# Layer 1 of a hybrid encoder: PSUM evacuation of the S5 states split over two engines, and the scan cut into two halves of the groups

## The chip, the cores and the metric

The kernel runs on one core of one Trainium2 chip. The metric is the device time of one execution in microseconds (us); lower is better. Engines are named as in the profile: PE (matmul), PEld (its weight loads), DVE (vector), ACT (scalar), POOL and SP (here they mostly issue DMAs).

## What is computed

Two encoder layers over 272 tokens (256 and 16 meta tokens) of width 2048. Each has a mixer and a channel mixer (layer 0 a dense SwiGLU, layer 1 a top-2-of-8 mixture of experts). The mixer projects the normed input once, gives one part to latent attention of 8 heads and the other, `u`, to a bidirectional S5, whose core is

```
bu = jnp.einsum('gpc,blgc->blgp', b_bar, u_c)
def combine(left, right):
    a_l, b_l = left
    a_r, b_r = right
    return a_r * a_l, a_r * b_l + b_r
_, h = lax.associative_scan(combine, (a, bu), axis=1, reverse=reverse)
return jnp.real(jnp.einsum('gcp,blgp->blgc', c, h))
```

for 64 groups of 16 channels with 64 complex states, forward and backward. Its output goes through a gelu and a gate (GLU); both halves are normed and multiplied by `w_out`.

## The kernel before

All weights stream through SBUF in 128x1024 blocks (`raw`), which ACT rounds into `wh` and DVE subtracts into `wl`; each product is three matmuls (XH·wh, XL·wh, XH·wl).

The S5 in chunks: tokens come in 68 chunks of 4. `ssm_x` (L1033) makes for each of 32 pairs of groups (one from each half of the 64) the state inputs of all chunks by matmuls into one PSUM bank, and ACT copies them into the tile `X` [128 partitions, 67 chunks, re/im, 64 groups] in two instructions: the forward direction in partitions 0 to 63, the backward one, in reversed order of chunks, in 64 to 127. `ssm_scan` (L1076) then steps over the 66 chunks: four DVE instructions a step, two products with `L8` (the transition, prepared at the end of `prep`, L811) and two adds into `X[:, s]`. `ssm_h` (L1094) copies states out of `X` in 16 pieces H (ACT the forward half, DVE the backward half), `ssm_y` (L1270) multiplies them on PE with the output weights (24 matmuls for each of 8 row tiles T, in the order 0, 4, 1, 5, 2, 6, 3, 7), copies the result `y` out, transposes it on PE, and ACT makes the gelu and its rounded copy for the GLU. Both `ssm_h` and `ssm_y` wait for the flag `("scan", l)`, `ssm_h` also for `("att", l)`, the end of attention. In the trace almost all these tiles are called `fa` (one arena); `L` is `L8`, `ra` the rounded arena.

Order of the work: nothing is reordered on the chip; each engine runs its queue in order. The queues are written by a planner when the kernel is built. A main generator (`mixer`, L1386) writes the big matmuls of a layer: projections of `u` (8 row tiles), of q and kv, the heads, then the first half of `w_out` (`w_out`, L1596, 16 blocks of 24 matmuls, each with two DVE instructions `tmpr` and `h`), then it waits for the flag `("Y", l)`, and only then the GLU. Side generators (attention and the `ssm_` functions) are let in between by a model of the engines' clocks: a scan step is written only when

```
return self.m.t["DVE"] < self.now() + self.lead[w]
```

that is, when DVE's planned time is less than 1200 ns ahead of PE's, and one that waits for data only when the planned time of the data is past. So the more planned DVE work there is, the later the scan's last step stands relative to the main matmuls.

Of the kernel before, what the change touches and what calls it, by code (L numbers as in the profile page):

```python
# [12 lines left out]
AF = mybir.ActivationFunctionType  # L13
OP = mybir.AluOpType
# [50 lines left out]

def rows(t, off, ap):
    return bass.AP(tensor=t.tensor, offset=t.offset + off, ap=ap)


class Arena:  # L70
# [461 lines left out]
class Kern:  # L532
# [278 lines left out]
    def prep(self, l, F):  # L811
# [103 lines left out]
        for b in range(0, len(src), 8):  # L915
            bank = yield from self.grab()
            ps = bank.rearrange("p (s g) -> p s g", g=64)
            part = src[b:b + 8]
            for i, (s, m, r) in enumerate(part):
                nc.tensor.transpose(ps[:, i, :], s, idn)  # L920
            i = 0
            while i < len(part):
                j = i
                while j + 1 < len(part) and part[j + 1][2] == part[i][2] and (part[j + 1][1] < n1) == (part[i][1] < n1):
                    j += 1
                m0, r, n = part[i][1], part[i][2], j - i + 1
                if m0 < n1:
                    nc.vector.tensor_copy(self.Wp[0:64, r, m0:m0 + n], ps[0:64, i:i + n])
                    hi = n1 - m0
                    nc.vector.tensor_copy(self.Wp[64:128, r, hi - n + 1:hi + 1], ps[64:128, i + n - 1:(i - 1 if i else None):-1])  # L930
                elif r == 0:
                    nc.vector.tensor_copy(self.L8[:, 0, 0], ps[:, i])
                    nc.vector.tensor_copy(self.L8[:, 0, 1], ps[:, i])
                else:
                    nc.vector.tensor_copy(self.L8[:, 1, 1], ps[:, i])
                    nc.vector.tensor_scalar(self.L8[:, 1, 0], ps[:, i], -1.0, None, op0=OP.mult)
                i = j + 1
            self.drop(bank)
            yield f"prep{l}"
# [93 lines left out]
    def ssm_x(self, l, F):  # L1033

        nc, st = self.nc, self.st
        X = st["X"]
        st["xu"] = {}

        def inputs():
            for qb in range(4):  # L1040
                yield lambda: qb - st["xb"] < 2
                yield self.has("u", l, qb)
                yield self.has("u", l, qb + 4)
                yield max(self.rdy(self.uscr[l][qb]), self.rdy(self.uscr[l][qb + 4]))
                u = self.load_u(l, qb)
                st["xu"][qb] = u, self.rdy(u)

        st["xb"] = 0
        self.s.add(inputs())
        for qb in range(4):  # L1050
            yield lambda: qb in st["xu"]
            u, t = st["xu"][qb]
            yield t
            for q in range(0, 8, VG):
                yield lambda: len(st["vq"]) > 0
                v, t = st["vq"].pop(0)
                yield t
                for i in range(VG):
                    g = qb * 8 + q + i
                    bank = yield from self.grab()  # L1060
                    ps = bank[:, :4 * NC].rearrange("p (r h s) -> p r h s", r=2, h=2)
                    for r in range(2):
                        nc.tensor.matmul(ps[:, r].rearrange("p h s -> p (h s)"), v[:, i, r],
                                         u[:, q + i].rearrange("p h s -> p (h s)"), start=True, stop=True)
                    if i == VG - 1:
                        st["vn"] += 1
                    yield None
                    nc.scalar.activation(X[0:64, :, :, g::NQ].rearrange("p s r h -> p r h s"),
                                         ps[0:64, :, :, 0:NC - 1], AF.Copy)
                    nc.scalar.activation(X[64:128, ::-1, :, g::NQ].rearrange("p s r h -> p r h s"),  # L1070
                                         ps[64:128, :, :, 1:NC], AF.Copy)
                    self.drop(bank)
            st["xb"] = qb + 1
        self.flags.add(("X", l))

    def ssm_scan(self, l, F):  # L1076
        nc, st = self.nc, self.st
        TT = nc.vector.tensor_tensor
        yield self.has("X", l)
        X = st["X"]  # L1080
        yield self.rdy(X.ap)
        t1, t2 = F.get([2, NG], top=True), F.get([2, NG], top=True)
        for s in range(1, NC - 1):
            TT(t1.ap, self.L8[:, 0], X[:, s - 1], op=OP.mult)
            TT(t2.ap, self.L8[:, 1], X[:, s - 1, ::-1], op=OP.mult)
            TT(X[:, s], X[:, s], t1.ap, op=OP.add)
            TT(X[:, s], X[:, s], t2.ap, op=OP.add)
            yield f"scan{l}"
        t1.free()
        t2.free()  # L1090
        st["tX"] = self.rdy(X.ap)
        self.flags.add(("scan", l))

    def ssm_h(self, l, F):  # L1094
# [10 lines left out]
        for T in TORD:  # L1105
            for a in (0, 4):
                yield lambda: n - st["hn"] < 2
                t = rh.next()
                yield self.s.m.clear(t)
                g = 8 * T + a  # L1110
                nc.scalar.activation(t[0:64, :, :, 1:NC],
                                     X[0:64, :, :, g:g + 4].rearrange("p s r g -> p g r s"), AF.Copy)
                nc.vector.tensor_copy(t[64:128, :, :, 0:NC - 1],
# [1264 lines left out]
```

## Time and profile before

| | us |
|---|---|
| median of 3 runs (2504.59 to 2511.16) | 2509.04 |
| the profiled execution | 2510.87 |
| its span, first to last instruction | 2509.1 |
| PE busy in the span | 2426.2 |
| DVE busy | 1903.8 |
| ACT busy | 1397.2 |

The profiled execution's time is 1.8 us above its span and 1.8 us above the median. Busy PE is matmuls with modelled ends. In layer 1's mixer the state inputs are made until 1383 us of the span, the scan runs from 1383 to 1519.5, the softmax of attention from 1450, first half of `w_out` from 1514 with the S5 output inside it, GLU from 1591.

### The profile page before, as it was taken

The page shows a single profiled execution, that of the slowest core. Times are in us where ns is not written, and L with a number is a line of the kernel's source. Part 1 is how long each engine was busy: PE and PEld are TensorE (multiplying, and loading weights), DVE is VectorE, ACT ScalarE, POOL GpSimd, SP SyncE. Part 2 cuts the span into 40 slices and gives each one's busy share as a digit, 9 for nine tenths or more (in the row PEclk, how much of TensorE's full clock was granted, in tenths as well). Part 3 has the DMA queues.
Part 4 walks back from the last instruction along what each step waited for, and adds up shares of the span by engine and source line. Part 5 has one row for each costly group of instructions (what it writes and reads, how often), then busy time and mean ns, then how long its engine had stood idle before and what let it go on. Part 6 is the DMA issues. An engine that isn't in the chain of part 4 may idle for free. (4 is left out here: it accounts for less than half of the span.)

```text
span 2509.1 us, 42278 instructions
## 1 busy us (share of the span) xinstructions
PE 2426.2 (97%) x15930; PEld 2185.7 (87%) x15930; DVE 1903.8 (76%) x3250; ACT 1397.2 (56%) x1908; POOL 152.1 (6%) x263
## 2 busy tenths in 40 slices
PE   8889999999999999999999799999999999999997
PEld 6676699999999999999998768997888888888886
DVE  7788667787766666555663987758999999999997
ACT  4324656443333333333448457547777777877775
POOL 4400100011100000000011002000000000000000
PEclk9999999999999999999999999999999999999998
DMA  7842454568855655555565325667999999999995
GB/s 246 240 134 92 138 161 152 168 211 269 260 187 192 193 193 187 171 174 176 173 197 190 101 68 161 224 228 266 389 347 355 384 339 376 362 330 372 362 336 198
DMA packets 192807, 583.47 MB, mean 233 GB/s; under 512 B 36097, under 2 KB 48769, under 8 KB 191441
## 3 DMA queue, kind: packets, MB, share of 16 engines
q1 hardware_dynamic: 174802, 520.42, 59.5%
q0 software_dynamic: 17072, 58.03, 7.6%
q8 instruction: 127, 2.08, 0.3%
q10 hardware_dynamic: 720, 2.23, 0.2%
q14 instruction: 86, 0.70, 0.1%
HBM read 560.14 MB, written 22.54 MB: 232 GB/s over the span
## 5 line engine op out<-in xcount | busy, mean ns | idle before, releaser
L408 DVE TENSOR_TENSOR wl<-raw,wh 128x1024 fp32r<-128x1024 f32 (+1 forms) x559 | 667.6, 1203 | 223.3 <-ACT wh L408 199.3
L408 ACT ACTIVATE wh<-raw 128x1024 fp32r<-128x1024 f32 (+1 forms) x559 | 579.3, 1040 | 315.0 <-PE bank L408 221.4
L408 PE MATMUL bank<-XH,wh 128*128 128x272 f32 (+1 forms) x2160 | 637.8, 295 | 0.8 <-ACT tmpr L408 0.5
L408 PE MATMUL bank<-XH,wl 128*128 128x272 f32 (+1 forms) x2160 | 623.7, 289 | 5.2 <-DVE wl L408 5.2
L408 PE MATMUL bank<-XL,wh 128*128 128x272 f32 (+1 forms) x2160 | 622.1, 288 | 1.6 <-DVE XL L408 1.3
L408 PEld LDWEIGHTS bank<-XH,wl 128*128 128x128 f32 x2160 | 408.0, 189 | 6.5 <-DVE wl L408 6.5
L408 PEld LDWEIGHTS bank<-XH,wh 128*128 128x128 f32 x2160 | 408.6, 189 | 5.2 <-ACT tmpr L408 0.7
L408 PEld LDWEIGHTS bank<-XL,wh 128*128 128x128 f32 x2160 | 408.7, 189 | 2.7 <-DVE XL L408 2.2
L408 PE MATMUL bank<-ra,wh 128*128 128x272 f32 (+1 forms) x1792 | 342.6, 291 | 2.3 <-ACT wh L408 2.3
L408 PEld LDWEIGHTS bank<-ra,wh 128*128 128x128 f32 x1792 | 281.9, 189 | 7.7 <-issue 3.1
L408 PE MATMUL bank<-fa 128*68 128x64 f32 (+12 forms) x1892 | 254.9, 273 | 26.2 <-ACT fa L408 7.9
L408 DVE TENSOR_TENSOR fa<-fa 128x128 f32<-128x128 f32 (+9 forms) x687 | 236.2, 353 | 40.3 <-ACT fa L408 15.8
L408 PEld LDWEIGHTS bank<-fa 128*68 128x68 f32 (+6 forms) x1892 | 190.9, 157 | 84.8 <-issue 43.8
L408 PE MATMUL bank<-ra,wl 128*128 128x272 f32 (+1 forms) x896 | 257.3, 287 | 0.8 <-DVE wl L408 0.8
L408 ACT ACTIVATE fa<-bank 64x268 f32<-64x268 f32 (+9 forms) x313 | 159.4, 515 | 154.6 <-PE bank L408 128.0
L408 PE MATMUL bank<-wh,XH 128*128 128x512 f32 (+1 forms) x584 | 222.4, 381 | 0.7 <-ACT fa L408 0.4
L408 PE MATMUL bank<-wh,XL 128*128 128x512 f32 (+1 forms) x584 | 220.5, 378 | 0.0
L408 PE MATMUL bank<-wl,XH 128*128 128x512 f32 (+1 forms) x584 | 219.1, 375 | 0.0
L408 PE MATMUL bank<-wh,ra 128*128 128x512 f32 x552 | 185.2, 392 | 0.0
L408 PE MATMUL bank<-fa,raw 128*128 128x272 f32 x608 | 164.5, 408 | 8.9 <-ACT fa L408 8.9
L408 PEld LDWEIGHTS bank<-ra,wl 128*128 128x128 f32 x896 | 169.3, 189 | 1.0 <-DVE wl L408 1.0
L408 DVE TENSOR_TENSOR wl<-h,wh 128x1024 fp32r<-128x1024 f32 (+1 forms) x137 | 157.0, 1156 | 10.0 <-ACT wh L408 7.5
(128 smaller groups left out, 3213.1 us busy)
## 6 DMA issues: line engine op xcount, KB each, us to landing
raw<-w_dense SPq DMA_DIRECT2D x264, 512.0 KB, 3.5
raw<-w_mix SPq DMA_DIRECT2D x150, 512.0 KB, 3.4
raw<-w_moe_g SPq DMA_DIRECT2D x106, 512.0 KB, 5.4
h<-w_moe_g SPq DMA_DIRECT2D x80, 512.0 KB, 5.6
raw<-w_moe_d SPq DMA_DIRECT2D x73, 512.0 KB, 6.6
h<-w_moe_d SPq DMA_DIRECT2D x59, 512.0 KB, 6.3
raw<-w_moe_t SPq DMA_DIRECT2D x51, 384.0 KB, 4.2
h<-w_moe_t SPq DMA_DIRECT2D x44, 384.0 KB, 3.9
```

The costliest lines, as they stand in the source:

```text
L408: return f(*a, **k)
```

## The change

The 64 columns of `X` and `L8` get another order: 16 columns belong to one of the four quarters of the groups' pairs, so the first two quarters fill columns 0 to 31. `L8` is written in that order (layer 0 too), and `ssm_h` reads by it. In layer 1 DVE, instead of ACT, copies the backward half out of PSUM, and the scan is two passes over 32 columns each; the first may start when two quarters of `X` are there. Layer 0 keeps one pass and ACT alone.

```diff
@@ prep @@
-                    nc.vector.tensor_copy(self.L8[:, 0, 0], ps[:, i])
-                    nc.vector.tensor_copy(self.L8[:, 0, 1], ps[:, i])
+                    nc.vector.tensor_copy(by_use(self.L8[:, 0, 0]), by_half(ps[:, i]))
+                    nc.vector.tensor_copy(by_use(self.L8[:, 0, 1]), by_half(ps[:, i]))
...
@@ ssm_x @@
-                    nc.scalar.activation(X[0:64, :, :, g::NQ].rearrange("p s r h -> p r h s"),
+                    c = slice(qb * 16 + q + i, qb * 16 + 16, 8)
+                    nc.scalar.activation(X[0:64, :, :, c].rearrange("p s r h -> p r h s"),
                                          ps[0:64, :, :, 0:NC - 1], AF.Copy)
-                    nc.scalar.activation(X[64:128, ::-1, :, g::NQ].rearrange("p s r h -> p r h s"),
-                                         ps[64:128, :, :, 1:NC], AF.Copy)
+                    back = X[64:128, ::-1, :, c].rearrange("p s r h -> p r h s")
+                    if l:
+                        nc.vector.tensor_copy(back, ps[64:128, :, :, 1:NC])
+                    else:
+                        nc.scalar.activation(back, ps[64:128, :, :, 1:NC], AF.Copy)
                     self.drop(bank)
             st["xb"] = qb + 1
+            self.flags.add(("X", l, qb))
@@ ssm_scan @@
-        t1, t2 = F.get([2, NG], top=True), F.get([2, NG], top=True)
-        for s in range(1, NC - 1):
-            TT(t1.ap, self.L8[:, 0], X[:, s - 1], op=OP.mult)
-            TT(t2.ap, self.L8[:, 1], X[:, s - 1, ::-1], op=OP.mult)
-            TT(X[:, s], X[:, s], t1.ap, op=OP.add)
-            TT(X[:, s], X[:, s], t2.ap, op=OP.add)
-            yield f"scan{l}"
+        n = NG // 2 if l else NG
+        for a in range(0, NG, n):
+            yield self.has("X", l, (a + n) // 16 - 1)
+            X, L8 = st["X"][:, :, :, a:a + n], self.L8[:, :, :, a:a + n]
+            yield self.rdy(X)
+            t = [F.get([2, n], top=True) for _ in range(2)]
+            for s in range(1, NC - 1):
+                for i, x in enumerate((X[:, s - 1], X[:, s - 1, ::-1])):
+                    nc.vector.tensor_tensor(t[i].ap, L8[:, i], x, op=OP.mult)
+                for x in t:
+                    nc.vector.tensor_tensor(X[:, s], X[:, s], x.ap, op=OP.add)
+                yield f"scan{l}"
...
@@ ssm_h @@
-                g = 8 * T + a
+                g = T % 4 * 16 + T // 4 * 8 + a
```

The queues of SP and POOL are the same before and after. DVE has 296 instructions more (32 copies, 264 of the scan), ACT 32 fewer, PE as many as before; PE's queue differs only in layer 1's mixer. The lines move by 9 (L408 is now L417). Two places:

**PE, first half of layer 1's `w_out`** (`XH,wh`, `XL,wh`, `XH,wl` are its matmuls, 128x256; `fa 68x64` those of `ssm_y`, `cst,fa 128x68` its transposes, `ra,wh` the GLU). Before:

```order
L408 MATMUL bank_66<-XH,wh_101 128x256
L408 MATMUL bank_66<-XL,wh_101 128x256
L408 MATMUL bank_66<-XH,wl_104 128x256
L408 MATMUL bank_69<-fa 68x64 x6
L408 MATMUL bank_70<-cst,fa 128x68 x4
L408 MATMUL bank_66<-XH,wh_101 128x256
```

After, the end of `w_out`'s last block and the beginning of what follows it:

```order
L417 MATMUL bank_66<-XH,wh_101 128x256
L417 MATMUL bank_66<-XL,wh_101 128x256
L417 MATMUL bank_66<-XH,wl_104 128x256
L417 MATMUL bank_71<-fa 68x64 x24
L417 MATMUL bank_69<-fa 68x64 x12
L417 MATMUL bank_70<-cst,fa 128x68 x4
L417 MATMUL bank_69<-fa 68x64 x12
L417 MATMUL bank_68<-fa 68x64 x12
```

and the end of that stretch:

```order
L417 MATMUL bank_68<-fa 68x64 x12
L417 MATMUL bank_70<-fa 68x64 x12
L417 MATMUL bank_69<-cst,fa 128x68 x4
L417 MATMUL bank_70<-fa 68x64 x12
L417 MATMUL bank_71<-cst,fa 128x68 x4
L417 MATMUL bank_67<-ra,wh_102 128x256 x2
L417 MATMUL bank_67<-ra,wl_105 128x256
```

Before, `ssm_y`'s 192 matmuls stand in sixes between threes of `w_out`, from its fourth block on, and 210 matmuls of `w_out` follow them. Now all 384 matmuls of `w_out` come first, then all of `ssm_y` with nothing between, then the GLU.

**DVE at the end of the scan** (`fa<-L_93,fa` are a step's two products, `fa<-fa` its two adds; `tmpr` and `h` belong to a block of `w_out`; `MEMSET fa` and `COPY fa<-fa` are the beginning of `ssm_h`). Before, the last step and what follows:

```order
L408 TENSOR_TENSOR wl_106<-raw_97,wh_103 128x1024
L408 TENSOR_TENSOR fa<-L_93,fa 128x128 x2
L408 TENSOR_TENSOR fa<-fa 128x128 x2
L408 MEMSET fa 128x544 x2
L408 RECIPROCAL fa<-fa 128x256
L408 TENSOR_TENSOR tmpr<-bank_66,fa 128x256
L408 TENSOR_TENSOR h<-h,tmpr 128x256
```

After, the last two blocks of `w_out` with the steps between:

```order
L417 TENSOR_TENSOR tmpr<-bank_65,fa 128x256
L417 TENSOR_TENSOR h<-h,tmpr 128x256
L417 TENSOR_TENSOR wl_106<-raw_97,wh_103 128x1024
L417 TENSOR_TENSOR fa<-L_93,fa 128x64 x2
L417 TENSOR_TENSOR fa<-fa 128x2x32 x2
L417 TENSOR_TENSOR tmpr<-bank_66,fa 128x256
L417 TENSOR_TENSOR h<-h,tmpr 128x256
L417 TENSOR_TENSOR fa<-L_93,fa 128x64 x2
```

The last step stood ahead of the RECIPROCAL that opens `w_out`'s DVE work. Now 105 of the 132 half-width steps stand ahead of that RECIPROCAL, 12 stand one by one behind blocks 4 to 15 of `w_out`, and 15 in a row behind the last one, ahead of the MEMSET. Of the 105, 22 stand ahead of DVE's work on the second block of the q projection (the row that ran at 1379.58 us, behind which the scan used to begin), with 29 of the 32 PSUM copies; 83 steps and 3 copies stand from there to the RECIPROCAL, where all 66 full-width steps stood.

## Rows read from the trace of the kernel before

**Rows 1.** The page, part 1: busy us (share of the span) xinstructions, by engine.

```profile
PE 2426.2 (97%) x15930; PEld 2185.7 (87%) x15930; DVE 1903.8 (76%) x3250; ACT 1397.2 (56%) x1908; POOL 152.1 (6%) x263
```

**Rows 2.** Busy time of each engine by stretch of layer 1's mixer: stretch, its length, busy us (and instructions) of PE, PEld, DVE, ACT, POOL, granted TensorE clock as a share of 2.4 GHz, DMA share, GB/s.

```profile
1330.00:1383.00 53.00, 49.65 (x400) 48.44 (x399) 18.09 (x20) 44.52 (x64) 7.63 (x13) 1.00 0.56 182
1383.00:1450.00 67.00, 52.52 (x339) 47.78 (x339) 61.88 (x169) 28.10 (x47) 0.00 (x0) 0.95 0.33 108
1450.00:1500.00 50.00, 46.42 (x242) 31.81 (x242) 41.71 (x158) 30.36 (x82) 0.00 (x0) 1.00 0.21 68
1500.00:1516.00 16.00, 15.62 (x49) 9.12 (x49) 14.38 (x60) 6.94 (x18) 1.77 (x3) 0.58 0.02 5
...
1523.00:1568.50 45.50, 43.25 (x543) 42.04 (x542) 28.93 (x44) 34.13 (x45) 7.36 (x11) 1.00 0.55 171
```

**Rows 3.** What PE waited for from 1383 to 1520 us: waiting engine and tile, releaser, us in total, times, longest; the rows released by DVE.

```profile
PE bank L408 <- DVE wl L408: 6.7, 5, 2.2
PE bank L408 <- DVE fa L408: 5.5, 3, 2.4
PE bank L408 <- DVE XL L408: 4.0, 4, 1.9
```

**Rows 4.** The same from 1300 to 1383 us, the first row.

```profile
PE bank L408 <- ACT fa L408: 3.8, 5, 1.0
```

**Rows 5.** DVE in order of time near the scan's beginning: start, us, instruction, count (instructions in a row are merged): one step of 128 elements and the next one's products.

```profile
1384.06 0.49 DVE L408 TENSOR_TENSOR fa<-L,fa 128x128 f32<-128x128 f32 x2
1384.47 0.61 DVE L408 TENSOR_TENSOR fa<-fa 128x128 f32<-128x128 f32 x2
1385.12 0.49 DVE L408 TENSOR_TENSOR fa<-L,fa 128x128 f32<-128x128 f32 x2
```

**Rows 6.** DVE's instructions of the whole span by form: shapes, count, then busy us and mean ns of one, then idle time before them. The first is a scan step's add, the third a plain copy out of PSUM, the fourth the copies of `ssm_h`, which read `X` in steps of one chunk.

```profile
L408 DVE TENSOR_TENSOR fa<-fa 128x128 f32<-128x128 f32 x264 | 76.0, 288 | 4.6
...
L408 DVE TENSOR_TENSOR fa<-fa 128x16 f32<-128x16 f32 x6 | 1.0, 172 | 0.1
...
L408 DVE COPY fa<-bank 128x256 f32<-128x256 f32 x8 | 3.3, 413 | 0.0
...
L408 DVE COPY fa<-fa 64x536 f32<-64x536 f32 x32 | 24.3, 780 | 1.1 <-PE bank L408 0.4
```

**Rows 7.** ACT by form from 1320 to 1383 us, the copies of the states out of PSUM (all 64 of layer 1).

```profile
L408 ACT ACTIVATE fa<-bank 64x268 f32<-64x268 f32 x64 | 41.1, 642 | 8.0 <-PE bank L408 7.0
```

**Rows 8.** PE in order of time: the first matmul of `w_out`'s first half, a sum of squares among them, and the first matmul of the GLU.

```profile
1514.23 0.38 PE L408 MATMUL bank<-XH,wh 128*128 128x256 f32 x1
...
1517.46 0.70 PE L408 MATMUL bank<-fa,ones 128*128 128x256 f32 x2
...
1591.37 0.40 PE L408 MATMUL bank<-ra,wh 128*128 128x256 f32 x2
```

**Rows 9.** DVE in order of time behind `ssm_y`, while PE does `w_out` alone: one block's `tmpr` and `h`, and the next block's `tmpr`.

```profile
1571.69 0.43 DVE L408 TENSOR_TENSOR tmpr<-bank,fa 128x256 f32<-128x256 f32 x1 [0.64 <-PE bank L408]
1572.15 0.42 DVE L408 TENSOR_TENSOR h<-h,tmpr 128x256 f32<-128x256 f32 x1
...
1574.53 0.42 DVE L408 TENSOR_TENSOR tmpr<-bank,fa 128x256 f32<-128x256 f32 x1 [0.64 <-PE bank L408]
```

**Rows 10.** DVE at the scan's end: the last step's adds and the memsets of `ssm_h`.

```profile
1518.86 0.61 DVE L408 TENSOR_TENSOR fa<-fa 128x128 f32<-128x128 f32 x2
1519.54 1.08 DVE L408 MEMSET fa<- 128x544 f32 x2
```

**Rows 11.** ACT, the first H copy.

```profile
1520.08 1.18 ACT L408 ACTIVATE fa<-fa 64x536 f32<-64x536 f32 x1 [0.46 <-DVE fa L408]
```

**Rows 12.** PE inside `ssm_y`: a run of its matmuls (24 records are the 12 matmuls of one H, two records each) and the transposes of one T.

```profile
1533.31 1.64 PE L408 MATMUL bank<-fa 128*68 128x64 f32 x24
...
1537.45 0.42 PE L408 MATMUL bank<-cst,fa 68*128 68x68 f32 x4
```

**Rows 13.** ACT through one T of `ssm_y`: y copy, H copy, gelu, rounded copy, then (left out, 1.14 us) another H copy, next y copy.

```profile
1540.59 0.59 ACT L408 ACTIVATE fa<-bank 68x512 f32<-68x512 f32 x1 [0.54 <-PE bank L408]
1541.08 1.15 ACT L408 ACTIVATE fa<-fa 64x536 f32<-64x536 f32 x1
1543.13 0.63 ACT L408 ACTIVATE fa<-bank 128x256 f32<-128x256 f32 x1 [0.90 <-PE bank L408]
1543.79 0.42 ACT L408 ACTIVATE ra<-fa 128x256 fp32r<-128x256 f32 x1
...
1545.40 0.59 ACT L408 ACTIVATE fa<-bank 68x512 f32<-68x512 f32 x1 [0.15 <-PE bank L408]
```

**Rows 14.** Busy time by stretch, columns as in rows 2: two pieces of attention.

```profile
1460.00:1470.00 10.00, 9.16 (x49) 6.11 (x47) 8.71 (x31) 6.35 (x18) 0.00 (x0) 1.00 0.24 73
1500.00:1510.00 10.00, 10.00 (x23) 5.11 (x23) 8.62 (x37) 3.97 (x12) 0.00 (x0) 0.50 0.00 0
```

**Rows 15.** PE behind a wait of 2.34 us that ended at 1397.32: two matmuls of one form.

```profile
1398.97 0.43 PE L408 MATMUL bank<-XH,wh 128*128 128x272 f32 x1
...
1401.06 0.29 PE L408 MATMUL bank<-XL,wh 128*128 128x272 f32 x1
```

**Rows 16.** Sum over 1600 to 1750 us, the stretch from the GLU to the first experts, columns as in rows 2.

```profile
sum 150.00, PE 141.71 PEld 129.49 DVE 104.02 ACT 83.58 POOL 4.78; mean PE 47.24 PEld 43.16 DVE 34.67 ACT 27.86 POOL 1.59
```

More of the change, by code (lines that the diff above doesn't have):

```diff
@@ L67, in rows, with by_half, by_use @@
     return bass.AP(tensor=t.tensor, offset=t.offset + off, ap=ap)
+def by_half(t):
+    return t.rearrange("p (h q i) -> p h q i", h=2, q=4)
+def by_use(t):
+    return t.rearrange("p (q h i) -> p h q i", h=2, q=4)
 class Arena:
@@ L931, in prep @@
                 elif r == 0:
-                    nc.vector.tensor_copy(self.L8[:, 0, 0], ps[:, i])
-                    nc.vector.tensor_copy(self.L8[:, 0, 1], ps[:, i])
-                else:
-                    nc.vector.tensor_copy(self.L8[:, 1, 1], ps[:, i])
-                    nc.vector.tensor_scalar(self.L8[:, 1, 0], ps[:, i], -1.0, None, op0=OP.mult)
+                    nc.vector.tensor_copy(by_use(self.L8[:, 0, 0]), by_half(ps[:, i]))
+                    nc.vector.tensor_copy(by_use(self.L8[:, 0, 1]), by_half(ps[:, i]))
+                else:
+                    nc.vector.tensor_copy(by_use(self.L8[:, 1, 1]), by_half(ps[:, i]))
+                    nc.vector.tensor_scalar(by_use(self.L8[:, 1, 0]), by_half(ps[:, i]), -1.0, None, op0=OP.mult)
                 i = j + 1
@@ L1058, in ssm_x @@
                 for i in range(VG):
-                    g = qb * 8 + q + i
                     bank = yield from self.grab()
@@ L1077, in ssm_scan @@
         nc, st = self.nc, self.st
[L1078 to L1081, printed above, removed]
-        t1, t2 = F.get([2, NG], top=True), F.get([2, NG], top=True)
-        for s in range(1, NC - 1):
-            TT(t1.ap, self.L8[:, 0], X[:, s - 1], op=OP.mult)
-            TT(t2.ap, self.L8[:, 1], X[:, s - 1, ::-1], op=OP.mult)
-            TT(X[:, s], X[:, s], t1.ap, op=OP.add)
-            TT(X[:, s], X[:, s], t2.ap, op=OP.add)
-            yield f"scan{l}"
-        t1.free()
-        t2.free()
-        st["tX"] = self.rdy(X.ap)
+        n = NG // 2 if l else NG
[10 more added lines that the diff above has]
+                yield f"scan{l}"
+            for x in t:
+                x.free()
+        st["tX"] = self.rdy(st["X"].ap)
         self.flags.add(("scan", l))
```

## The prediction, made before the changed kernel ran

> **What bounds the kernel now.** I read the page's first part first: PE is busy for 97% of the span [rows 1], so a change can win only where PE idles, and it loses whatever idle time it adds to PE. The next view is the table by stretch [rows 2]; the reader is to see where layer 1's mixer leaves PE idle: 3.35 us while the states are made (1330 to 1383), then 14.48, 3.58 and 0.38 us up to 1516, and 2.25 us in the stretch of `ssm_y` (1523 to 1568.5). The waits name the releasers: from 1383 to 1520 DVE ended 6.7 + 5.5 + 4.0 = 16.2 us of PE's waits [rows 3], and before that ACT, which copies the states out, ended 3.8 [rows 4]. From 1383 to 1516 DVE is busy 118 of 133 us, with the scan in it. So the change attacks two real waits. What it does to the order behind them weighs more: `ssm_y` ran inside `w_out`, and PE was busy 43.25 of those 45.5 us [rows 2].
>
> **The prices.** A full-width step starts 1.06 us after the one before (1384.06 to 1385.12 [rows 5]), with four instructions. One of 128 elements takes 288 ns, one of 16 takes 172 [rows 6]: 1.036 ns an element over a fixed 155 ns, so one of 64 takes 222. Four times 66 ns less makes a half-width step 0.79 us. It can't cost more than the full one, 1.06, nor less than half, 0.53. A pass over all groups is 66 x 1.06 = 70 us before, 132 x 0.79 = 104 us after: DVE gets 34 us more. The row nearest in kind to DVE's copy out of PSUM is 413 ns for 256 elements [rows 6]; ACT's takes 642 for 268 [rows 7], as ACT pays for the stepped side; DVE's copies of `ssm_h`, stepped too, take 780 for 536, close to the plain rate. I take 0.45 us, between 0.41 and 0.64: 32 x 0.45 = 14 us more on DVE, 32 x 0.64 = 20.5 us less on ACT. The different column order of `L8` and of the copies keeps their counts and sizes; I cost it at nothing.
>
> **Term 1, the states.** ACT's share per bank falls from two copies to one, so the 3.8 us [rows 4] can go. On DVE, 29 copies (13 us) and 22 steps (17 us) now stand before the point of 1379.58; some eight of the copies fall before 1330, so the stretch holds 18 + 27 = 45 of 53 us of DVE work. That fits, though a copy can stand behind a step or a `wl` and hold a bank. I take -2, with ends -3.8 (all of the wait) and +6 (a bank held 0.8 us by a step for eight groups).
>
> **Term 2, projections and attention.** Where 66 steps (70.0 us) stood, 83 half-width ones stand (65.6 us), with 3 copies more (1.4) and without the memsets (1.1): DVE has 4 us less of 118. Of the 16.2 us that PE waits for DVE I let 2 go: -2. Ends: -4, all of it passed on, and 0.
>
> **Term 3, the scan's tail and `ssm_y`.** PE's queue now holds all of `w_out`'s first half, then all of `ssm_y`, then the GLU. `w_out` begins at 1514.23 [rows 8]; a block takes 2.84 us (1571.69 to 1574.53 [rows 9]); 16 blocks are 45.4, with 0.7 for the sum among them [rows 8], so PE is through at 1560.3. The steps behind blocks 4 to 15 fit: 0.42 + 0.42 + 1.22 + 0.79 with the `wl` is 2.85 of 2.84. After the last `tmpr` and `h` (1.0 with the hand-over) DVE has 15 steps left: 15 x 0.79 = 11.9, to 1573.2, while PE stands, since nothing else is in its queue. The last add to ACT's first H copy was 0.61 (1519.47 to 1520.08) and the copy 1.18 [rows 10, 11]; with a hand-over the first matmul of `ssm_y` is at 1575.2.
>
> From there `ssm_y` runs alone. Per T PE has 2 x 1.64 for the matmuls and 0.42 for the transposes [rows 12], 3.70; ACT has 0.59 + 1.15 + 0.63 + 0.42 + 1.14 = 3.93 [rows 13]; DVE, two copies of 0.78 and one 0.42, has slack. They wait for each other: the transposes wait for the y copy and stand behind the next H's matmuls, and ACT's gelu waits for them. I walk that ring: two sets of matmuls, the transposes, one y copy and a hand-over of 0.1 make 4.4 us, between 3.70 (PE alone) and 4.81 (1540.59 to 1545.40 with `w_out` in between [rows 13]). First T: two sets, y copy and hand-overs, 4.2 us, and 1.7 more because PE comes out of a long wait: behind 2.34 us of waiting a matmul took 0.43, 2 us later 0.29 [rows 15], starts 0.23 and 0.12 apart. Then 7 x 4.4 = 30.8, and the last T's transposes, gelu, rounded copy and subtraction, 0.42 + 0.63 + 0.42 + 0.42 with 0.5 of hand-overs, 2.4. The GLU starts at 1575.2 + 5.9 + 30.8 + 2.4 = 1614.3, not at 1591.37 [rows 8]: **+22.9 us**. Ends: cycles at 3.70 and 4.81, -4.9 and +2.9.
>
> What stands behind the GLU is unchanged and PE-bound, so the delay stays. Sum: -2 - 2 + 22.9 = +18.9 on the profiled 2510.87; against the median, 1.8 us lower, 2509.0 + 18.9 = **2528 us**.
>
> **A rule against the change.** In the trace two independent products take 0.49 us together where one alone takes 0.285, so the second starts before the first has ended [rows 5]. The Trainium skill, "VectorE: DVE Perf Modes", section "The DRAIN you can't avoid", says the next operation does not start until the pipeline is empty, and its rules for authors say to keep the number of operations low. By that rule the doubled count of scan instructions would cost more than I take; the trace bears the overlap out instead, for these products at least.
>
> **Rivals.**
> - *Steps dearer*: the four instructions don't overlap at half width and take 4 x 0.222 = 0.89 us, and PSUM copies take ACT's 0.64. Term 2 gets 83 x 0.10 = 8 us and term 3 15 x 0.10 = 1.5, term 1 turns to +6 because the copies hold banks: 2528 + 18 = 2546. Against it the overlap in rows 5, for it the short adds that depend on each other (0.61 for two). 0.13.
> - *`ssm_y` at the half clock*: PE at 1.2 GHz doubles its share of the ring, 4 x 1.64 + 0.84 + 0.69 = 8.1, so 7 x 3.7 = 26 us more: 2554. For it: the tail of attention, where PE stands between short bursts, ran at 0.50 [rows 14]. Against it: at 1460 to 1470 PE, with its weight loads busy 6.1 of 10 us, had 1.00, and alone in `ssm_y` it would have 3.7 of 4.4. The Trainium skill, "TensorE: Matmul & The Clock Gate", "Part 1: The HAM clock gate", says that the low level is the default and sustained work releases it; the rows fit that. 0.10.
> - *The delay is taken back later*: from 1600 to 1750 PE idles 150 - 141.7 = 8.3 us [rows 16]; if all of it were late data that now has time to come, the time is 2520. Nothing shows that these waits are for data. 0.08.
> - *Not slower*: a half-width step costs half, 0.53 us. Then term 2 frees 70 - 44 = 26 us of DVE, and all 16.2 us of PE's waits for DVE go (14 more than taken), ACT's wait goes too (2), the tail is 15 x 0.26 = 4 shorter, and the ring runs at PE's 3.70 (5 less): 2528 - 25 = 2503. It decides below about 0.6 us a step. Against it stands the fixed part in rows 6: 172 ns for 16 elements. 0.06.
> - *The change doesn't do what it says*: the first pass does start earlier, the second ends later, so the scan as a whole ends later; that is my forecast.
>
> **Chances.** Forecast 0.63, the rivals 0.13, 0.10, 0.08 and 0.06. Its own range is 2509 + 18.9 - 4.9 - 1.8 - 2 = 2519 to 2528 + 2.9 + 2 + 8 = 2541. To leave out no more than 0.2 I go down to 2516 and up to 2547, which takes in the dearer steps and the delay taken back; the half clock and the other side stay out. A difference of 0.3%, 7.5 us, is about what a measurement of this kernel can tell from none: faster 0.04 (half of the last rival and some luck), same 0.07, slower 0.89.
>
> **What would show it.** Right: scan instructions `fa<-L` 128x64, 0.22 us each; ACT's copies of 64x268 halved; a gap on PE of about 15 us between the last XH matmul of `w_out`'s first half and the first 128x64 one, ended by DVE or ACT `fa`; then some 37 us in which PE is busy well under 90% with no XH matmul; GLU 20 us later. Wrong: a gap under 8 us, `ssm_y` in under 30 us, or a stretch 1383 to 1516 shorter by 10 us.

## The result: slower by 0.86%

| | before | after |
|---|---|---|
| median, us | 2508.87 (6 runs, 2504.59 to 2512.82) | 2530.82 (6 runs, 2528.78 to 2536.22) |
| ratio to before, 95% interval | | 1.0086 [1.0071, 1.0102], that is +18 to +26 us |
| the profiled execution, us | 2510.87 | 2528.78 |
| its span, us | 2509.1 | 2527.0 |

The forecast was 2528, slower. The profiled execution is the shortest of the six, 2 us under their median, so what its trace adds up to (+17.9) stands a little under the difference of the medians (+22).

The page's first part, to be read beside [rows 1]: PE does the same work in a longer span, DVE is busy 46 us more (the forecast had 34 for the scan and 14 for the copies), ACT 23 less.

```profile
PE 2424.0 (96%) x15930; PEld 2187.6 (87%) x15930; DVE 1949.5 (77%) x3546; ACT 1374.6 (54%) x1876; POOL 152.6 (6%) x263
```

The table by stretch of layer 1's mixer, the same columns as [rows 2]. The last two stretches are new: the gap, and `ssm_y` by itself.

```profile
1330.00:1383.00 53.00, 48.64 (x395) 47.66 (x394) 44.94 (x131) 27.02 (x38) 7.40 (x12) 1.00 0.55 172
1383.00:1450.00 67.00, 54.92 (x337) 49.26 (x336) 61.42 (x209) 27.48 (x48) 0.00 (x0) 0.92 0.37 117
1450.00:1500.00 50.00, 47.27 (x247) 32.04 (x245) 41.21 (x191) 31.41 (x88) 0.00 (x0) 1.00 0.17 55
1500.00:1516.00 16.00, 12.94 (x77) 10.99 (x78) 15.23 (x65) 8.10 (x15) 5.54 (x9) 0.89 0.51 153
1555.10:1569.80 14.70, 0.03 (x1) 0.02 (x1) 13.52 (x67) 1.42 (x2) 0.00 (x0) 0.60 0.12 37
1569.80:1607.50 37.70, 31.15 (x415) 30.32 (x416) 13.87 (x22) 27.88 (x38) 7.49 (x11) 0.88 0.34 100
```

DVE's and ACT's work moves as planned (26.9 us more and 17.5 less from 1330 to 1383), but for PE the stretches up to 1500 look as before: where the change was to help, its busy time moves by 1 to 2.4 us up or down. From 1555.1 to 1569.8 PE does nothing while DVE is busy 13.5 of 14.7 us, and in the 37.7 us after that PE is busy 31.2.

PE in order of time (compare [rows 8, 12]): the first matmul of `w_out`, its last one, the first of `ssm_y`, one cycle of it, the last transposes, the first of the GLU.

```profile
1507.47 0.58 PE L417 MATMUL bank<-XH,wh 128*128 128x256 f32 x1
...
1554.85 0.28 PE L417 MATMUL bank<-XH,wl 128*128 128x256 f32 x1
1569.81 7.10 PE L417 MATMUL bank<-fa 128*68 128x64 f32 x72 [14.67 <-ACT fa L417]
...
1600.32 0.42 PE L417 MATMUL bank<-cst,fa 68*128 68x68 f32 x4
1600.57 1.64 PE L417 MATMUL bank<-fa 128*68 128x64 f32 x24
1603.21 1.66 PE L417 MATMUL bank<-fa 128*68 128x64 f32 x24 [1.00 <-ACT fa L417]
1604.71 0.42 PE L417 MATMUL bank<-cst,fa 68*128 68x68 f32 x4
...
1607.29 0.47 PE L417 MATMUL bank<-cst,fa 68*128 68x68 f32 x4 [0.68 <-ACT fa L417]
1607.56 0.48 PE L417 MATMUL bank<-ra,wh 128*128 128x256 f32 x2
```

The wait of 14.67 us is put down to ACT, whose H copy came last. DVE and ACT show who was late: behind the last block's `h` DVE goes through 15 steps in a row (first and last shown), then the memsets, and ACT's H copy had itself waited 15.11 us for DVE.

```profile
1555.63 0.42 DVE L417 TENSOR_TENSOR h<-h,tmpr 128x256 f32<-128x256 f32 x1
1555.97 0.35 DVE L417 TENSOR_TENSOR fa<-L,fa 128x64 f32<-128x64 f32 x2
1556.24 0.48 DVE L417 TENSOR_TENSOR fa<-fa 128x64 f32<-128x64 f32 x2
1556.76 0.36 DVE L417 TENSOR_TENSOR fa<-L,fa 128x64 f32<-128x64 f32 x2
...
1567.29 0.48 DVE L417 TENSOR_TENSOR fa<-fa 128x64 f32<-128x64 f32 x2
1567.83 1.09 DVE L417 MEMSET fa<- 128x544 f32 x2
```

```profile
1568.38 2.10 ACT L417 ACTIVATE fa<-fa 64x536 f32<-64x536 f32 x2 [15.11 <-DVE fa L417]
```

The prices, by form (columns of [rows 6]): the adds and products of a half-width step, and DVE's copies out of PSUM.

```profile
L417 DVE TENSOR_TENSOR fa<-fa 128x64 f32<-128x64 f32 x264 | 58.5, 222 | 4.5
...
L417 DVE TENSOR_TENSOR fa<-L,fa 128x64 f32<-128x64 f32 x264 | 47.1, 220 | 2.3
...
L417 DVE COPY fa<-bank 64x268 f32<-64x268 f32 x32 | 18.3, 638 | 9.1 <-ACT fa L417 8.8
```

### The profile page after: what moved, and what is told of

Its sections match the earlier page's. It is cut to its first block, busy times and chain, and to the rows that moved or that the text cites. A ratio compares the mean times of both kernels' runs of the same rounds, so it can differ in the third digit from the quotient of the medians.

```text
span 2527.0 us, 42564 instructions
## 1 busy us (share of the span) xinstructions
PE 2424.0 (96%) x15930; PEld 2187.6 (87%) x15930; DVE 1949.5 (77%) x3546; ACT 1374.6 (54%) x1876; POOL 152.6 (6%) x263
## 5 line engine op out<-in xcount | busy, mean ns | idle before, releaser
L417 DVE TENSOR_TENSOR wl<-raw,wh 128x1024 fp32r<-128x1024 f32 (+1 forms) x559 | 667.6, 1202 | 191.7 <-ACT wh L417 186.4
L417 ACT ACTIVATE wh<-raw 128x1024 fp32r<-128x1024 f32 (+1 forms) x559 | 579.7, 1040 | 332.5 <-PE bank L417 246.6
L417 PE MATMUL bank<-XH,wh 128*128 128x272 f32 (+1 forms) x2160 | 636.6, 295 | 0.8 <-ACT tmpr L417 0.5
L417 PE MATMUL bank<-XH,wl 128*128 128x272 f32 (+1 forms) x2160 | 625.0, 289 | 5.3 <-DVE wl L417 5.3
L417 PE MATMUL bank<-XL,wh 128*128 128x272 f32 (+1 forms) x2160 | 623.7, 289 | 1.5 <-DVE XL L417 1.3
L417 PEld LDWEIGHTS bank<-XH,wl 128*128 128x128 f32 x2160 | 409.6, 190 | 6.2 <-DVE wl L417 6.2
L417 PEld LDWEIGHTS bank<-XH,wh 128*128 128x128 f32 x2160 | 410.1, 190 | 5.3 <-ACT tmpr L417 0.7
L417 PEld LDWEIGHTS bank<-XL,wh 128*128 128x128 f32 x2160 | 410.1, 190 | 2.4 <-DVE XL L417 1.9
L417 PE MATMUL bank<-ra,wh 128*128 128x272 f32 (+1 forms) x1792 | 341.8, 291 | 2.3 <-ACT wh L417 2.3
L417 PE MATMUL bank<-fa 128*68 128x64 f32 (+12 forms) x1892 | 252.8, 275 | 48.7 <-ACT fa L417 25.6
L417 DVE TENSOR_TENSOR fa<-fa 128x64 f32<-128x64 f32 (+11 forms) x819 | 256.7, 321 | 41.4 <-ACT fa L417 13.8
L417 PEld LDWEIGHTS bank<-ra,wh 128*128 128x128 f32 x1792 | 281.5, 189 | 7.7 <-issue 3.1
L417 PEld LDWEIGHTS bank<-fa 128*68 128x68 f32 (+6 forms) x1892 | 191.4, 160 | 104.9 <-issue 47.2
L417 PE MATMUL bank<-ra,wl 128*128 128x272 f32 (+1 forms) x896 | 257.2, 287 | 1.9 <-DVE wl L417 1.9
L417 ACT ACTIVATE fa<-bank 64x268 f32<-64x268 f32 (+9 forms) x281 | 138.1, 501 | 162.9 <-PE bank L417 141.7
L417 PE MATMUL bank<-wh,XH 128*128 128x512 f32 (+1 forms) x584 | 221.9, 380 | 0.7 <-ACT fa L417 0.4
L417 PE MATMUL bank<-wh,XL 128*128 128x512 f32 (+1 forms) x584 | 219.8, 376 | 0.0
L417 PE MATMUL bank<-wl,XH 128*128 128x512 f32 (+1 forms) x584 | 218.5, 374 | 0.0
L417 PE MATMUL bank<-wh,ra 128*128 128x512 f32 x552 | 185.5, 393 | 0.0
L417 PE MATMUL bank<-fa,raw 128*128 128x272 f32 x608 | 163.9, 407 | 9.1 <-ACT fa L417 9.1
L417 PEld LDWEIGHTS bank<-ra,wl 128*128 128x128 f32 x896 | 169.3, 189 | 2.3 <-DVE wl L417 2.3
L417 DVE TENSOR_TENSOR wl<-h,wh 128x1024 fp32r<-128x1024 f32 (+1 forms) x137 | 157.0, 1156 | 9.9 <-ACT wh L417 7.7
```

The costliest lines, as they stand in the source:

```text
L417: return f(*a, **k)
```

## The experiments

Two theories stood at first. **Order**: the loss is the order behind attention, PE's wait for the end of the scan and `ssm_y` running alone. **Amount**: the loss is the extra DVE work, wherever it stands. Results are ratios to the kernel before on the same chip. In lead2600, before_lead2600, per_half, few_steps and pool_half the condition under which the planner gives `ssm_h` its memory is changed too (not shown in the diffs below); no run tests that by itself. few_steps and short leave out part of the scan and serve only to price it.

| kernel | ratio, 95% interval | us against before |
|---|---|---|
| y_late | 1.0030 [1.0018, 1.0041] | +7.5 |
| two_engines | 1.0003 [0.9991, 1.0014] | +1 |
| halves | 1.0074 [1.0062, 1.0086] | +18.6 |
| lead2600 | 1.0133 [1.0116, 1.0149] | +33 |
| per_half | 1.0014 [1.0002, 1.0026] | +3.5 |
| two_y3 | 1.0006 [0.9992, 1.0019] | +1.5 |
| before_lead2600 | 1.0064 [1.0049, 1.0080] | +16 |
| few_steps | 0.9969 [0.9958, 0.9981] | -8 |
| short | 0.9993 [0.9979, 1.0007] | -2 |
| te_lead1050 | 0.9977 [0.9965, 0.9989] | -6 |
| before_lead1050 | 0.9985 [0.9974, 0.9995] | -4 |
| pool_half | 1.0057 [1.0040, 1.0075] | +14 |

**y_late.** The kernel before with only the order of `ssm_y` changed.

```diff
@@ mixer, behind w_out's first half @@
+        self.flags.add(("wo", l))
@@ ssm_y @@
         yield self.has("scan", l)
+        if l:
+            yield self.has("wo", l)
```

> The kernel before, with one thing changed: ssm_y of layer 1 may write its matmuls only when all 16 blocks of w_out's first half are written, so that PE's queue there reads as in the changed kernel (384 matmuls of w_out, then ssm_y alone, then the GLU). The scan stays at full width and ends before w_out. Order theory (the loss is PE's wait for the end of the scan plus ssm_y running alone): there is no wait for the scan here, and ssm_y alone takes the 4.39 us a T that it took in the changed kernel; w_out 1514.2 + 46.1 = 1560.3, ssm_y 8 x 4.39 = 35.1 and 1.2 for its first y copy, the GLU at 1596.6 instead of 1591.4: +5, some 2514 us. Rival (the extra DVE instructions are the price, the order is not): nothing was added, 2509, GLU within 1 us of before.

Measured 2515.93 us, +7.5 (4.5 to 10.3). PE of this kernel: the first matmuls of `ssm_y`, a cycle, the GLU.

```profile
1562.19 4.59 PE L408 MATMUL bank<-fa 128*68 128x64 f32 x72
...
1579.51 1.66 PE L408 MATMUL bank<-fa 128*68 128x64 f32 x24 [0.99 <-ACT fa L408]
...
1583.90 1.66 PE L408 MATMUL bank<-fa 128*68 128x64 f32 x24 [1.00 <-ACT fa L408]
...
1597.02 0.48 PE L408 MATMUL bank<-ra,wh 128*128 128x256 f32 x2
```

The GLU starts 5.65 us later than at 1591.37 [rows 8], 1.0 of which was already there when the mixer began. The cycle is the changed kernel's, 4.39 us, with 1 us of it PE's wait for ACT. So order alone, with not one instruction added, costs 5 us in the trace and 7.5 by the medians. The first 72 records took 4.59 us here and 7.10 behind the changed kernel's gap.

**halves and two_engines.** Each takes one part of the change away: the split of the copies, or the two passes.

```diff
@@ halves: ssm_x @@
-                    if l:
-                        nc.vector.tensor_copy(back, ps[64:128, :, :, 1:NC])
-                    else:
-                        nc.scalar.activation(back, ps[64:128, :, :, 1:NC], AF.Copy)
+                    nc.scalar.activation(back, ps[64:128, :, :, 1:NC], AF.Copy)
@@ two_engines: ssm_scan @@
-        n = NG // 2 if l else NG
+        n = NG
```

> The changed kernel with ACT making both copies out of PSUM again; the two passes stay. 112 of the 132 steps stand ahead of w_out, 12 among its blocks, 8 behind the last one; PE's queue there is the changed kernel's. Order theory: the tail of the scan behind w_out is 8 steps of 0.79 = 6.3 us instead of 15 (11.8), so PE's gap is 14.7 - 5.5 = 9.2 us; ssm_y alone as in the changed kernel; the states lose what the split gave them, 1 to 2 us: some 2527 us. Rival (the split of the copies is what costs): 2509 to 2515. Rival (the number of scan instructions alone counts): as the changed kernel, 2531.

> The changed kernel with the scan of layer 1 in one pass over all 64 columns again, so only the column order and DVE's copies of the backward half remain. All 66 steps stand ahead of w_out and ssm_y is among w_out's blocks from the second block on. Order theory: no wait for the scan, no lonely ssm_y, ACT's 3.8 us wait at the states partly gone, X complete earlier by up to 10 us and the scan with it: -1 to -6, some 2505 us. Rival (the copies on DVE hold banks behind other DVE work and cost PE): +3 to +8 at the beginning of the scan, 2512 to 2517. Rival (the doubled instruction count of the scan is the whole price): back at 2507 to 2509.

Measured 2527.36 and 2509.73. In halves the tail behind `w_out` is 8 steps, and PE's gap is what 7 steps less leave of it:

```profile
1569.11 7.00 PE L417 MATMUL bank<-fa 128*68 128x64 f32 x72 [9.14 <-ACT fa L417]
```

9.14 us where 9.2 was expected; a step is worth 0.79 us of PE. In two_engines the order of before comes back and the loss goes. That the split of the copies helps (2505) isn't borne out by the time: +1 us, between -2 and +4.

**lead2600 and before_lead2600.** The lead, which says how early a step may be written, raised in the changed kernel and, to understand the first, in the kernel before.

```diff
-        "prep1": 400.0, "v1": 800.0, "w1": 700.0, "scan1": 1200.0, "gate": 2125.0}
+        "prep1": 400.0, "v1": 800.0, "w1": 700.0, "scan1": 2600.0, "gate": 2125.0}
```

> The changed kernel with a larger lead for the scan (a step is written while DVE's planned time is less than 2600 ns ahead of PE's, not 1200; the states' rings are given memory a little later in the plan, which moves nothing on the chip). All 132 half-width steps now stand ahead of w_out, and ssm_y is among w_out's blocks from the second one on. Nothing is taken away: as many DVE instructions as in the changed kernel. Order theory: the gap of 14.7 us and the lonely ssm_y go, 23 us; the 27 steps that come earlier (21 us of DVE) go into the projections and attention, where DVE has about 15 us idle from 1383 to 1516, so 6 to 12 us of new PE waits: 2505 to 2516, taken 2511. Rival (the extra DVE instructions cost wherever they stand, 34 us of DVE of which 22 reach the end): no better than the changed kernel, 2527 to 2535.

Measured 2540.34, +33: order theory, as I had put it, missed by 29 us. The gap was gone; the loss had moved ahead of `w_out`, which began 21 us later than before. What PE waited for from 1383 to 1520 (beside [rows 3]):

```profile
PE bank L417 <- DVE wl L417: 11.6, 7, 3.9
PE bank L417 <- DVE fa L417: 6.8, 2, 3.7
PE bank L417 <- DVE XL L417: 6.3, 4, 2.8
```

Was it the amount of DVE work there, or its place?

> The kernel before with the lead of the scan at 2600 instead of 1200, nothing else on DVE changed: 66 full-width steps, all ahead of w_out as they were. Its purpose is the 31 us that the same lead cost in lead2600. If those were the amount of DVE work ahead of w_out (27 half-width steps, 21 us more, where DVE is already the bound), nothing is added here: 2507 to 2513. Rival (it is the place: with the larger lead steps stand ahead of the softmax's and the norms' short DVE work, and PE waits longer for each): 2517 to 2530.

Measured 2527.52, +16, with no work added; the same view of this kernel:

```profile
PE bank L408 <- DVE wl L408: 12.8, 8, 3.3
PE bank L408 <- DVE fa L408: 6.6, 2, 3.4
PE bank L408 <- DVE XL L408: 5.0, 2, 4.5
```

So about half of lead2600's loss comes with the larger lead alone, that is, with the place of the steps (ahead of the short DVE work that PE waits for). The other 17 us lie between before_lead2600 and lead2600, which differ in the two passes (34 us more of DVE, all ahead of `w_out`), the column order and the copies on DVE. The traces show them in another form. From the first matmul of the q projection to the first of `w_out`, PE waits 16.2 us for DVE in the kernel before, 24.4 in before_lead2600 and 27.8 in lead2600; in the same stretches PE is busy 132.0, 135.0 and 151.3 us for nearly the same matmuls (772, 772 and 781 records), at a granted clock of 0.93, 0.90 and 0.83 of 2.4 GHz. The place shows as waits, the rest mostly as matmuls at the lower clock. That the added DVE work is what leaves PE at that clock is likely but not shown.

**per_half.** All DVE work of the change stays; only the flag of the scan is given per pass.

```diff
@@ ssm_scan, at the end of a pass @@
+            self.flags.add(("scan", l, a // n))
@@ ssm_h, ssm_y @@
-        yield self.has("scan", l)
+        yield self.has("scan", l, 0)
@@ ssm_h @@
         for T in TORD:
+            if T % 4 > 1:
+                yield self.has("scan", l)
```

> The changed kernel (split copies, two passes, the same lead), where the end of the first pass is announced by itself: ssm_h and ssm_y may do the four row tiles 0, 4, 1, 5, which use columns 0 to 31 alone, as soon as the first pass and attention are done. (The scan's temporaries of layer 1 get memory of their own, so that the rings fit.) 103 steps stand ahead of w_out, 29 among its first eight blocks, none behind it; ssm_y is spread over w_out in two pieces. Order theory: PE's gap of 14.7 us and the lonely ssm_y go, although DVE has as many instructions as in the changed kernel; w_out begins 6.8 us earlier than before, as there, and PE loses some 3 us among the first tiles, where ssm_y stands densely: 2503 to 2509, taken 2505. Rival (DVE's 34 us more of scan must come out at the end wherever a part of them stands): 2520 to 2531.

Measured 2514.02, +3.5 (0.5 to 6.5): 18 of the 22 us come back, but not the 5 below before that were taken. Amount, as it was put (2520 to 2531), falls. From the start of `w_out` to that of the GLU it took 85.0 us, where it took 77.1 before; PE waits some 6 us there, most of it in waits like these, at the beginning of a run of `ssm_y`, for which the profile names no releaser. In DVE's rows a copy of H ends 0.10 us before each of the two:

```profile
1518.04 0.75 DVE L417 COPY fa<-fa 64x536 f32<-64x536 f32 x1
...
1518.89 0.92 PE L417 MATMUL bank<-fa 128*68 128x64 f32 x12 [1.67 <-issue]
...
1526.52 0.76 DVE L417 COPY fa<-fa 64x536 f32<-64x536 f32 x1
...
1527.38 0.92 PE L417 MATMUL bank<-fa 128*68 128x64 f32 x12 [2.41 <-issue]
```

Ahead of each copy stand a `wl` and steps of the second pass in DVE's queue. So the second pass, no longer a wall behind `w_out`, still seems to hold up `ssm_y` by delaying the copies of H; the profile doesn't name them, so this is a reading of the order in time.

**short, few_steps and two_y3.** Is there a gain ahead of `w_out`, as the one profile has it (1507.47 against 1514.23)?

```diff
@@ short: ssm_scan of the changed kernel @@
-            for s in range(1, NC - 1):
+            for s in range(1, NC - 1 if a == 0 else NC - 28):
@@ few_steps: ssm_scan of the kernel before @@
-        for s in range(1, NC - 1):
+        for s in range(1, NC // 2 if l else NC - 1):
@@ two_y3: w_out of two_engines (ssm_y waits for "wo" as in y_late) @@
+            if half == 0 and m == 3:
+                self.flags.add(("wo", l))
```

> The changed kernel with the last 27 of the second pass's 66 steps left out (those that stood among and behind w_out's blocks; half of the groups' states are then not scanned to their end). The 105 steps ahead of w_out and all else before it stand as in the changed kernel; behind it there is no scan, and ssm_y is spread over w_out from its sixth block on. So its time is that of the changed kernel's part ahead of w_out, with the order of before behind it. If that part gained what the forecast says (4 us) or what the one profile showed (6.9 us): 2505 or 2502, taken 2504. Rival (the gain ahead of w_out in the profile is scatter between executions; the kernels with the split copies and one pass came out level with before): 2509.

> The kernel before with the last 33 of the 66 steps of layer 1's scan left out (its states are then not scanned beyond chunk 33): 35 us less DVE work between 1383 and w_out, everything else kept. If the amount of DVE work sets PE's waits there (16.2 us of them end by DVE), most of them go: -10 to -14, 2495 to 2499. Rival (PE waits for chains of short DVE work, not for the scan): -1 to -5, 2504 to 2508.

> The kernel two_engines (split copies, one full-width pass), with ssm_y held until three blocks of w_out are written, as it stood before the change. In two_engines w_out began 6.95 us earlier than before, the GLU only 4.7. If that loss is ssm_y's early start (its first tiles wait for ACT's and DVE's copies of H: 1.0, 1.3 and 1.0 us on PE), the GLU now begins 6 to 7 us earlier than before and the time is 2505 to 2508. Rival (the loss has another cause, or the clock behind the GLU takes it): 2509 to 2511.

short measured 2509.61, -2 (-5 to +2): no gain that the runs can tell from none. few_steps measured 2502.98, -8 (-11 to -5), between its two expectations: 35 us of DVE work are worth 8 us of PE (from the q projection to `w_out` its trace is 7.5 us shorter). two_y3 measured 2511.76, level with two_engines: the expectation of 2505 to 2508 fell. It showed something else. By the edit the two kernels have the same queues up to `w_out`'s second block, and yet its RECIPROCAL began at

```profile
1513.58 1.75 DVE L417 RECIPROCAL fa<-fa 128x256 f32<-128x256 f32 x1
```

in two_engines and at

```profile
1517.02 1.75 DVE L417 RECIPROCAL fa<-fa 128x256 f32<-128x256 f32 x1
```

in two_y3, 3.4 us apart, although two_engines had entered the mixer 1.9 us later: 5.3 us between the same instructions. The rows of PE say where. In two_y3 PE waits 2.55 us for the DMA that brings the rearranged `u` back from a scratch buffer, `uscr`, at a point where two_engines does not wait:

```profile
1336.43 1.25 PE L417 MATMUL bank<-fa 128*128 128x136 f32 x4 [2.55 <-DMA fa<-uscr]
```

The matmuls right behind it take twice as long as two_engines' (1.25 us for four, 0.62 to 0.63 there), at the lower clock, so that 4.1 us of the distance arise here. From 1371 us to `w_out` the two kernels keep the same distance within 0.1 us. So most of this scatter comes from where the states are made, not from the scan or attention, and one profile's advance in that stretch proves nothing.

Behind it the traces agree better. From the first matmul of the q projection to the first of `w_out` the kernel before takes 151.3 us and y_late, whose queues are the same up to there, 152.5; with the split copies it is 146.8 in the changed kernel, 149.1 in short, 148.3 in two_engines, 147.8 in two_y3 and 147.1 in per_half, and with the two passes alone 148.5 in halves, one trace each. That is 2 to 6 us less each time, the sign that the forecast gave to its second term. From the mixer's first matmul to the q projection it is 68.1, 66.6 and (halves) 69.6 without the split and 62.7 to 68.5 with it: no gain that can be told from the scatter.

**te_lead1050 and before_lead1050.** If place costs when the lead is larger, a smaller lead may gain, as long as the scan still ends in time. The edit is the line above with 1050, in two_engines and in the kernel before.

> The kernel two_engines (split copies, one full-width pass) with a lead of 1050 instead of 1200: steps stand a little later among attention's short DVE work, 65 of 66 still ahead of w_out, ssm_y spread from the eighth block on. The larger lead cost 17 us in the kernel before without adding work, so the place of the steps in attention counts; if that goes on below 1200, -2 to -6: 2504 to 2508. Rival (at 1200 the steps already stand where PE does not feel their place): 2509 to 2511.

> The kernel before with a lead of 1050 instead of 1200 and nothing else: ACT makes both copies, one full-width pass, 64 of its 66 steps ahead of w_out and two among its blocks, ssm_y spread from the tenth block on. te_lead1050, which has the split copies too, was 5.3 us faster than before. If the place of the steps alone did that, as much here: 2503 to 2507. If it needs the split copies (the states complete earlier, so that the scan can begin earlier): 2508 to 2511.

Measured 2505.26, -6 (-9 to -3), and 2506.61, -4 (-7 to -1): both faster than both kernels of the change. Most of it is the lead, which needs no split; what the split adds isn't told apart from none. PE's waits for DVE from 1383 to 1520 in te_lead1050 add up to 12.1 us, where [rows 3] have 16.2 (before_lead1050: 14.5):

```profile
PE bank L417 <- DVE XL L417: 4.9, 4, 1.8
PE bank L417 <- DVE fa L417: 4.0, 2, 2.0
PE bank L417 <- DVE wl L417: 3.2, 3, 1.6
```

**pool_half.** The two passes side by side on two engines.

```diff
@@ ssm_scan @@
+            self.s.add(half(0, "POOL", pool))       # columns 0 to 31, gpsimd.tensor_tensor
+            yield from half(n, "DVE", dve)          # columns 32 to 63
+            yield lambda: len(done) == 2
```

> The changed kernel with the first pass (columns 0 to 31) on POOL and the second on DVE, side by side; both stand ahead of w_out, ssm_y is spread over w_out from the second block on. POOL was idle from 1383 to 1500. DVE then has 66 half-width steps (52 us) where before it had 66 full-width ones (70): by few_steps, where 35 us less DVE work gave 7.6 us, the 18 us less are worth 4 us: 2505, if a step on POOL takes less than about 2.4 us (160 us from 1355 on for 66 steps) and does not slow DVE. Rival (a step on POOL takes longer than 2.4 us, or DVE's instructions run slower beside POOL's, and ssm_y waits for the scan): each 0.1 us of a step is 6.6 us, so 2515 to 2560.

Measured 2525.74, +14: the rival, and of its clauses the second is seen. POOL was fast enough (a step began every 1.35 us where nothing came between); DVE was slowed. By form, POOL's products and adds, then DVE's adds and products of a step and a copy out of PSUM:

```profile
L1115 POOL TENSOR_TENSOR fa<-L,fa 128x64 f32<-128x64 f32 x132 | 57.3, 455 | 5.9 <-DVE fa L417 1.2
L1115 POOL TENSOR_TENSOR fa<-fa 128x64 f32<-128x64 f32 x132 | 46.6, 353 | 5.2
```

```profile
L417 DVE TENSOR_TENSOR fa<-fa 128x64 f32<-128x64 f32 x132 | 36.5, 276 | 2.3
L417 DVE TENSOR_TENSOR fa<-L,fa 128x64 f32<-128x64 f32 x132 | 31.9, 281 | 1.1
...
L417 DVE COPY fa<-bank 128x256 f32<-128x256 f32 x8 | 3.3, 415 | 0.0
```

An add takes 276 ns where it took 222 with POOL idle; the copy out of PSUM stays at 413 to 415. DVE's half of the scan so kept it busy 36.5 + 31.9 = 68.4 us, about the 70 that the whole scan took before: moving half of it to POOL took nothing off DVE. That explains why nothing was gained, not the whole loss. PE's waits for DVE from the q projection to `w_out` are 20.2 us (16.2 before), and there is a cause that the expectation left out: POOL also issues the DMAs through `uscr`, now with scan instructions between them in its queue, and PE waited for them from 1300 to 1383 us

```profile
PE bank L417 <- DMA fa<-uscr: 6.4, 3, 3.4
```

where it waited 0.5 us before and 2.7 in two_engines. How the 14 us divide stays open.

## Why the prediction was right, step by step

- *The prices.* A half-width instruction was put at 222 ns and a step at 0.79 us; measured 220 to 222, and 0.79 from step to step (1555.97 to 1556.76). The line through two widths in [rows 6] was enough. The copy out of PSUM was put at 0.45 us and took 0.638, the upper end: the row nearest in size and layout, ACT's 642 [rows 7], was the better guide, though no run tells whether the stepped side or something else makes DVE's copy dearer than the plain one. That DVE's work in 1330 to 1383 was put at 45 us and measured 44.9 is luck: 24 copies of 0.638 and 22 steps stand there, for 21 of 0.45 and 22, and the busy time of a stretch counts what overlaps once.
- *Term 1, the states (-2), and term 2, projections and attention (-2).* In the profile `w_out` begins 6.8 us earlier. The runs don't confirm it: short, which is the changed kernel up to there, is at -2, between -5 and +2. So -4 isn't excluded and isn't shown; the profile's 6.8 is partly scatter between executions. Term 2 has the right sign in six traces (2 to 6 us, above). Term 1 has not been seen. Its mechanism did happen, for ACT's 3.8 us of waits [rows 4] are gone, but others took their place in the same stretch, 1300 to 1383, where before there were 0.5 us for that DMA and none for DVE's `fa`:

```profile
PE bank L417 <- DMA fa<-uscr: 2.3, 3, 1.2
PE bank L417 <- DVE fa L417: 2.0, 2, 1.2
```

- *Term 3, the tail and `ssm_y` (+22.9).* From the start of `w_out` to that of the GLU it took 77.14 us before [rows 8], 100.09 after: +22.95. That this is the forecast to 0.05 us is luck, for the parts are less exact: `w_out` alone 47.7 us for 46.1 (its first matmuls ran at the lower clock, 0.41 us each for 0.28); DVE's 15 steps 11.86 for 11.9; PE's gap 14.67 for 14.9; `ssm_y` 37.75 for 39.1, with a cycle of 4.39 for 4.4. Two sizes inside `ssm_y` were off and partly cancelled. I had the GLU wait for the last T's gelu and its copies, 2.4 us; it starts 0.27 us after the last transposes start, with tiles that were ready. And I had not seen ACT's table load (1.28 us) ahead of the first gelu, behind which PE waits 1.99 us:

```profile
1577.11 1.28 ACT L417 ACT_TABLE_LOAD   x1
...
1580.83 1.92 PE L417 MATMUL bank<-fa 128*68 128x64 f32 x24 [1.99 <-ACT fa L417]
```

- *The split of the loss.* The changed kernel lost 22 us, y_late 7.5: the rest by the medians is 14.5. In the traces, from the start of `w_out` to that of the GLU, the two lie 17.95 us apart: the gap is 14.67 of it, `ssm_y` took 2.9 longer (2.5 in its first 72 records, behind the gap), `w_out` 0.4. The changed kernel came to `w_out` earlier, which takes some of that back. halves, with 7 steps fewer in the tail, shows the gap shorter by 7 x 0.79.
- *What stands behind.* PE-bound and unchanged: the delay was 16.2 us at the GLU and 15.7 at 2430. It grew to 17.9 at the end, by 0.9 us around 2458 and 0.7 behind it, as it did, by 1.6 in all, in two_engines, halves and lead2600; why, no run shows.
- *The rivals.* Dearer steps: fell, by 0.79. The half clock: `ssm_y` began at 1.2 GHz (granted 0.50 from 1569.8 to 1575, behind the gap) and was back at 2.4 by 1577; 72 records took 7.1 us instead of 4.59, so 2.5 us were lost where the rival had 26 and the forecast 1.7. The clock fell once more, to 0.71 from 1580 to 1585, behind the wait of 1.99 us, and was at 1.00 from 1590 on. The Trainium skill, "TensorE: Matmul & The Clock Gate", "Part 1: The HAM clock gate", says that the low level is the default and activity releases it; this trace agrees, with 0.50 behind the gap and 1.00 later on. Taken back later: fell, 15.7 of 16.2 us stayed. Not slower at 0.53 us a step: fell.
- *The rule on draining.* Two half-width products together take 0.36 us where one takes 0.22. The Trainium skill, "VectorE: DVE Perf Modes", "The DRAIN you can't avoid", has the next operation wait until the pipeline is empty, and in the same section lets one that isn't held start earlier; these products, by the measurement, are of the second kind, so the doubled count cost its fixed part (by the two-point estimate some 155 ns an instruction) and no more.

What the prediction did not ask: why more DVE work ahead of `w_out` was not the way out. before_lead2600 and lead2600 show that DVE's idle time there (some 15 of 133 us) can't be spent by writing steps earlier: they then stand ahead of short DVE work that PE waits for, and these waits grew from 16.2 to 24.4 and 27.8 us.

## What to carry to other kernels

Ask first what a change does to the order that a planner writes, and only then to the work: 34 us of extra DVE work pushed the end of a chain past a flag, and a stage that had run inside another ran alone behind it. That was most of the loss, with its gap of 14.7 us, the 2.5 us at the lower clock behind it and a lonely ring of some 5: with the same work and the result of each pass given by itself, 18 of the 22 us came back. A chain of steps cut in two must also give its result in two, or the consumers wait for both halves, and the fixed part of each instruction is paid twice (0.79 us for half of 1.06). And an engine's idle share is no reserve: moving steps earlier into attention cost 16 us without adding any, moving them a little later gained 4 to 6.

## What the hardware showed that was not expected

- DVE's products and adds with both operands in SBUF ran about a quarter longer beside POOL's (276 to 281 ns for 220 to 222), copies out of PSUM did not (415 for 413). The Trainium skill, "SBUF — State Buffer", "Who interferes with whom", says that a DVE instruction with two SBUF inputs contends with a GpSimd instruction that reads SBUF, and calls the shared ports an exclusive lock; which instructions are hit agrees (POOL is GpSimd). The mean loss of 54 to 61 ns is far from the length of a POOL instruction (353 to 455 ns), but it is not even: a step's two adds, 0.48 us with POOL idle, take that in some steps and half as much again in others:

```profile
1423.98 0.48 DVE L417 TENSOR_TENSOR fa<-fa 128x64 f32<-128x64 f32 x2
...
1425.06 0.75 DVE L417 TENSOR_TENSOR fa<-fa 128x64 f32<-128x64 f32 x2
```

- A wait of 14.67 us on PE cost 2.5 us more behind it, at the lower clock; one of 9.14 us (halves) 2.4, 7.00 us for the same 72 records. In y_late, where `ssm_y` followed without a wait, they took 4.59 us at a granted clock of 1.00.
- DVE's copy out of PSUM of 64x268 with a stepped destination costs as much as ACT's, 638 to 642 ns.
- Executions with the same instructions ahead of them stood 5 us apart at one point in the middle of the program, most of it by a wait for one DMA and the lower clock behind that. A gain of that size read from two profiles needs the times, or more traces, beside it.
